# A hybrid decoder layer on one core: the recording clock learns the shared SBUF port and a measured matmul time, and every rank is set anew

## The chip, the core and the metric

The kernel runs on one core of a Trainium2 chip. The core has five engines that work from queues of their own, each strictly in the order in which its instructions were recorded: TensorE (PE in the profile, with its weight loads as PEld), VectorE (DVE), ScalarE (ACT), GpSimd (POOL) and SyncE (SP), which issues the DMA transfers. The metric is the device time of one execution in microseconds. The kernel before takes 1484.05 us, the median of three runs from 1482.07 to 1484.79.

## The reference, cut to what matters

One decoder layer is computed for a new sequence of 1024 tokens and for 8 single tokens that continue cached sequences (the sample). All data are float32.

```
h    = rmsnorm(x)
proj = h @ w_in                                # 1024 x 2336
y_r  = rwkv7_mix(proj[:, :1696])               # 8 heads x 64, state update over time
y_a  = windowed attention(proj[:, 1696:])      # 8 query heads, 2 KV heads, window 128, sinks
x    = x + concat(y_r, y_a) @ w_out            # 1024 x 1024
hf   = rmsnorm(x)
x    = x + relu(hf @ w_ffn_up)**2 @ w_ffn_down # 1024 x 4096, 4096 x 1024
```

The outputs are x for all tokens, and the new states and caches of both groups.

## The kernel before, in words

**Precision by two parts.** Each float32 operand of a dense product is split into a rounded high part and the rest: `whi` is made by ACT from a loaded weight tile `wraw`, `wlo` is the difference, made by DVE or POOL; for activations the pairs are `hh`/`hl`, `xu`/`xu`, `uh`/`ul`. One dense product is three matmuls, high by high, low by high and high by low, summed in PSUM. Weights come in halves of 128 x 512; there are 480 halves in all, in one fixed order. A raw ring of five and rings of three for `whi` and `wlo` stand between the transfer and the matmul.

**Stages.** The 1032 columns (1024 prompt tokens, 8 sample tokens) are four chunks of 256 (the last 264). For each chunk the stream `s_dense` computes the input projection (its first part is `lora`, then `pairs` and `kvq`). Its results feed three other streams: the RWKV recurrence in eight blocks d (`s_front`, `s_solve`, `s_X`, `s_back`, `s_rest`), attention (`s_cons`, `s_attn`), and the sample. Then `s_dense` computes the output projection of chunk 0, a first pass of the FFN over chunk 0 alone (256 columns at a time, tiles `xu`), the output projection of chunks 1 to 3, and the remaining FFN over the other 776 columns in pieces of 388. Norm statistics of chunk 1 are taken early, by `ssq_rs`: ACT squares the tiles `xk`, POOL adds them up in `ssq`, PE reduces them in `ps_m`.

**What sets the order.** The kernel is written as some twenty Python generators (streams), each of which yields instructions one by one. `drive` merges them: at every step it takes, of all streams' next instructions, the one that can start first by a clock of its own; among those that would start on the same engine before it has ended, it takes the one whose stream has the lower rank. Ranks are the numbers in `R`, capped by `BOOST` when the dense stream can't start soon. The clock keeps one busy time per engine (`busy`), the time at which each tile was written (`wrote`) and read (`used`), a latency between each pair of engines (`LAT`), and for each kind of instruction a cost by its size (`tt`, `ts`, `stt`, `cp`, `act`, `burst` for matmuls). It also counts matmul work in ticks of 3.41 us (`ticks`) and doubles the cost of a matmul when the tick before had too little; `hot`, with `HOT` and `HOT0`, puts the dense stream ahead of all others until the current tick has its share. This clock decides nothing at run time: its result is five fixed queues. Where a stream may choose the engine for a `wlo`, it takes POOL when POOL's clock is behind DVE's by a set margin.

Semaphore waits follow from the data. An instruction that stands in a queue ahead of its time holds everything behind it on that engine.

Of the kernel before, what the change touches and what calls it, by code (L numbers as in the profile page):

```python
# [167 lines left out]
}  # L168


PAD = 0.0
HOT = 1
HOT0 = 0.2
MR = 2
TICK = 10.24 / 3
SWITCH = 0.095
# [3 lines left out]
DB = -0.5  # L180
LIM = dict(x=1, d=3, ffn=4, e=4, o=1, f=2, a=4, y=1)
SLACK = 2
BOOST = dict(s_wl=2.5, s_w=2.5, mix_load=2.51, s_hprep=0.5, s_evac=0, s_post=0.1, s_phase=0.0, norm=0, s_dense=2.5, s_cons=2.5, s_back=2.5, decode=1.5, s_attn=1.56, sample=99, s_rest=0.16, s_X=99)
R = dict(s_back=1.96, s_X=1.24, s_solve=7.69, s_front=0, s_rest=6.92, s_evac=0.9, s_hprep=3.47, s_post=1.1, s_cons=0, s_w=0, s_wl=0.19, s_attn=6.24, s_dense=8.9, s_phase=7.55, mix_load=5.54, sample=5.41, decode=1.62, blocks=8.2, norm=2.24)
WIN = []
ENG = lambda nc: (nc.tensor, nc.vector, nc.scalar, nc.gpsimd, nc.sync)

# [1 line left out]
def build(tc, A, stop=None):  # L189
    nc = tc.nc  # L190
    V, S, G, T, SP = nc.vector, nc.scalar, nc.gpsimd, nc.tensor, nc.sync
# [9 lines left out]
    busy = {V: 0.6, S: 0.6, G: 0.6, T: 0.6, SP: 0.6}  # L201
    wrote, used, slots = {}, {}, {}

    def tl(pl, shape, tag=None, bufs=1, name=None, dtype=F32):
        kw = dict(tag=tag, bufs=bufs) if tag else {}
        t = pl.tile(shape, dtype, name=name or tag, **kw)
        if tag:
            old = slots.setdefault((id(pl), tag), [])
            if len(old) == bufs:
                used[t.name] = slot_use(old.pop(0))  # L210
            old.append(t.name)
        return t

    def slot_use(n):
        u = dict(used.get(n, {}))
        if n in wrote:
            u[wrote[n][1]] = max(u.get(wrote[n][1], 0.0), wrote[n][0])
        return u
# [3 lines left out]
    def names(aps):  # L222
        out = []
        for a in aps:
            if not hasattr(a, "name"):
                continue
            if a.name in wide:
                o = a.offset
                out += [f"{a.name}/{c}" for c in (1, 2, 3) if o < QS[c][0] + QS[c][1] - NQ and QS[c][0] - NQ < o + size(a)]
            else:  # L230
                out.append(a.name)
        return out

    def op(e, cost, outs, ins, fn, rows=128):
        return e, cost, names(outs), names(ins), fn, rows

    ticks, dmas, shape = {}, [0.0], [None]
# [16 lines left out]
    def start(o):  # L254
        e, cost, outs, ins = o[:4]
        t = busy[e]
        for n in ins:
            w = wrote.get(n)
            if w:
                t = max(t, w[0] + LAT[w[1], e] + (PAD if e is T and w[1] is not T else 0.0))  # L260
        for n in outs:
            for f, w in used.get(n, {}).items():
                t = max(t, w + LAT[f, e])
        return t

    order = (T, V, S, G, SP)
    LAT = {(x, y): v for x, row in zip(order, ((0.0, .2, .27, .2, .2),
# [6 lines left out]
    def do(*ops):  # L274
        for o in ops:
            t = start(o)
            e, cost, outs, ins, fn, rows = o
            fn()
            end = finish(e, t, cost, rows)
            busy[e] = t + 0.5 if e is SP else end  # L280
            for n in outs:
                wrote[n] = (end, e)
                if e in (V, G, S):
                    used.setdefault(n, {})[e] = end
            for n in ins:
                used.setdefault(n, {})[e] = end

    def size(a):
        n = 1
        for d in a.shape[1:]:  # L290
            n *= d
        return n
# [6 lines left out]

    def tt(e, out, a, b, o, more=0.0):  # L300
        c = 0.07 + size(out) / 960 if e is V else 0.1 + size(out) / 450 if o != POW else 0.25 + size(out) / 6
        return op(e, c + more, [out], [a, b], lambda: e.tensor_tensor(out=out, in0=a, in1=b, op=o))  # L302

    def ts(e, out, a, s1, op0, s2=None, op1=None):
        kw = {} if op1 is None else dict(op1=op1)
        c = 0.07 + size(out) / 1300 if e is V else 0.1 + size(out) / 700
        return op(e, c, [out], [a, s1, s2],
                  lambda: e.tensor_scalar(out=out, in0=a, scalar1=s1, scalar2=s2, op0=op0, **kw))

    def stt(out, a, s, b, op0, op1):  # L310
        return op(V, (0.13 if hasattr(s, "name") else 0.07) + size(out) / 960, [out], [a, s, b],
                  lambda: V.scalar_tensor_tensor(out=out, in0=a, scalar=s, in1=b, op0=op0, op1=op1))  # L312

    def cp(e, out, in_):
        c = 0.07 + size(out) / 1200 if e is V else 0.1 + size(out) / 280
# [15 lines left out]
    def burst(*calls):  # L331


        t, free, now, first, active, outs, ins, fns = 0.0, {}, None, None, 0.0, [], [], []
        end = 0.0
        for call in calls:
            turn = len(call) == 3
            out, l, r = call[:3]
            start, stop, shared = (True, True, False) if turn else (*call[3:], False)[:3]
            k, m, n = l.shape[0], (size(r) if turn else size(l)), (l.shape[0] if turn else size(r))  # L340
            one = turn or r.dtype == F32R
            sh = (edge(k), edge(m))
            step = max(n * (1 if one else 2) / 2400 + (0.0112 if one and not turn else 0.003), m / 1200 + 0.004, 0.027)
            where = (l.start_partition() if sh[0] < 128 else 0, out.start_partition() if sh[1] < 128 else 0)
            if now != sh:
                if now is not None:
                    t = end + SWITCH
                now, free = sh, {}
            first = first or sh
            for _ in range(1 if one else 2):  # L350
                t = max(t + 0.007, free.get(where, 0.0))
                free[where] = end = t + step
                end = max(free.values())
            active += 0.055 if turn else (n / 2400 if one else 2 * n / 2400) * k / 128
            outs.append(out)
            ins += [l, r]
            fns.append((lambda o=out, i=l, d=r: T.transpose(o, i, d)) if turn else
                       (lambda o=out, a=l, b=r, x=start, y=stop, z=shared: T.matmul(o, a, b, start=x, stop=y, skip_group_check=z)))  # L358

        def run():  # L360
            for f in fns:
                f()
        return op(T, end, outs, ins, run, (first, now, active))
# [13 lines left out]
    streams, done = [], {}  # L377
# [22 lines left out]
    def drive():  # L400
        windows, over = list(WIN), {}
        while streams:
# [6 lines left out]
            i = int(busy[T] / TICK)  # L409
            hot = ticks.get(i, 0.0) >= 3060 / 2400 * min(1.0, HOT * (busy[T] / TICK - i) + HOT0)  # L410

            eff = {}

            def base(s):
# [3 lines left out]
                r = over.get(n, s[0])  # L418
                return min(BOOST.get(n, 99), r) if low else r

# [34 lines left out]
    pp_ = cm.__enter__()  # L455
    own, held, free_at = {}, {}, [{} for _ in range(7)]

    def get(kind, shape, name):
        yield lambda on=HOLD.get(kind): held.get(kind, 0) < LIM[kind] and len(own) < 7
        i = min((i for i in range(7) if i not in own.values()), key=lambda i: max(free_at[i].values(), default=0.0))  # L460
        t = tl(pp_, shape, f"b{i}", 1, name)
        own[t.name] = i
        kinds[t.name] = kind
        held[kind] = held.get(kind, 0) + 1
        return t
# [12 lines left out]
        free_at[i] = slot_use(t.name)  # L478

    def pt(shape, tag, name):  # L480
        return tl(pp_, shape, tag, 1, name)

    const = es.enter_context(pool("const", "left"))
    dram = es.enter_context(pool("dram", space=bass.MemoryType.DRAM))
# [89 lines left out]
    def s_wl():  # L574
        for j, (src, M) in enumerate(halves):
            yield lambda on="s_w": len(his) > j
            lo = tl(wp, [128, 4, M], "wl", WH, "wlo", F32R)
            e = G if busy[G] + 1.3 < busy[V] + 0.6 and not done.get("solving") else V
            yield tt(e, lo, raws[j], his[j].bitcast(F32), SUB)
            W.append((his[j], lo))  # L580

# [891 lines left out]
    def sample(sp):  # L1473
# [82 lines left out]
        for i, E in enumerate((V, G)):  # L1556
            St2 = tl(sp, [128, 4, 64], "p9t" if i else "St", 1)
            t3 = tl(sp, [128, 4, 64], name=f"t3_{i}")
            spawn(R["blocks"], blocks(i, E, St2, t3, kk, z, bvec, v, kn, r, sa, y))
        yield lambda: done.get("blk") == 2  # L1560
# [93 lines left out]
    def out_proj(c):  # L1654
# [3 lines left out]
        def consumer(m):  # L1658
            def f(n, ps):
# [8 lines left out]
                if m == 7:  # L1668
                    spawn(R["norm"], norm(c, ssq))
            return f  # L1670
# [85 lines left out]
    def s_phase():  # L1756
        yield lambda on="s_post": done.get(("kvq", 3)) and done.get("post", 0) == 56
        hs_.close()
        bm[0] = es.enter_context(pool("bm", "left"))
        spawn(R["sample"], sample(es.enter_context(pool("smp", "left"))))  # L1760
        yield lambda on="s_front": done.get(("front", 7))
        rfs.close()
        new_act0()
        done["acts"] = 1
        spawn(R["mix_load"], mix_load(0))
        yield lambda on="s_solve": done.get("xs")
        rss.close()
        yield lambda on="s_cons": done.get("cons") == 24
        dec = ExitStack()
        spawn(R["decode"], decode(dec.enter_context(pool("dec", "right"))))  # L1770
        yield lambda on="decode": done.get("decode")
# [6 lines left out]
        done["acts"] = 2  # L1778
        spawn(R["mix_load"], mix_load(1))
        yield lambda on="s_rest": done.get(("tail", 7))  # L1780
# [155 lines left out]
```

## Time and profile before

| | |
|---|---|
| median of the runs | 1484.05 us (1482.07 to 1484.79) |
| the profiled execution | 1479.39 us, span of its instructions 1477.6 us |
| PE busy | 1379.6 us, 93% of the span |
| DVE, ACT, POOL busy | 862.6, 659.0, 610.2 us |
| mean granted TensorE clock | 0.965 |
| moved by DMA | 168.14 MB, mean 114 GB/s |

The page gives busy time by engine, the groups of instructions that cost most, and for idle time what ended it. The view by stretches cuts the span into pieces and gives each engine's busy time in each, with the granted clock; the view in order of time gives single instructions with the idle time before them in square brackets. A matmul counts as busy from its issue to its modelled end, so that PE looks busy when matmuls follow each other without a gap.

### The profile page before, as it was taken

Reading aid. Unit: us, or ns where it says so; the run is one execution under the profiler, and the core shown is the slowest. Engines: PE = TensorE matmul, PEld = TensorE weight load, DVE = VectorE, ACT = ScalarE, POOL = GpSimd, SP = SyncE. Lnnn points to the kernel's source line nnn. Section 1 sums busy time; section 2 is a strip of 40 time slices with the busy share of each in tenths; the row PEclk is TensorE's granted clock in tenths of the full one; section 3 lists DMA queues with packets and bytes.
Section 4 is the critical chain, followed back from the end, with each engine's and each line's share of the span. In section 5 each row is a group of like instructions: output and inputs, shape, how many; then the busy total and the mean of one; then the engine's idle time right before and its main releaser. Section 6 shows DMA issues by size and latency. Waiting matters only on the chain.

```text
span 1477.6 us, 31265 instructions
## 1 busy us (share of the span) xinstructions
PE 1379.6 (93%) x11798; PEld 1294.2 (88%) x11798; DVE 862.6 (58%) x1962; ACT 659.0 (45%) x1519; POOL 610.2 (41%) x909
## 2 busy tenths in 40 slices
PE   6898988899879988989889999999999999999999
PEld 5887777688768877779889988999999999999998
DVE  3777777758777786689976588333323323233323
ACT  4557655565566545456445555323231313222221
POOL 4676445744765553245644443222212121222221
PEclk7998999899999998999999999999999999999999
DMA  6445335434432445258656665422222222222223
GB/s 193 139 121 137 111 87 131 121 95 113 121 109 77 104 114 165 71 154 271 199 165 187 186 206 151 116 60 62 65 58 65 65 58 65 65 65 62 60 58 101
DMA packets 140918, 168.14 MB, mean 114 GB/s; under 512 B 49321, under 2 KB 75457, under 8 KB 140751
## 3 DMA queue, kind: packets, MB, share of 16 engines
q1 hardware_dynamic: 140766, 166.14, 39.5%
q8 instruction: 93, 1.52, 0.4%
q14 instruction: 59, 0.48, 0.1%
HBM read 150.13 MB, written 14.35 MB: 111 GB/s over the span
## 4 chain that ended last, share of the span: by engine, by line
PE 64%; DVE 15%; POOL 6%; DMA 6%; issue 4%; ACT 3%; SPq 2%; DVEq 0%; POOLq 0%; ACTq 0%
PE ps_d L358 56%; DVE wlo L302 2%; SPq L372 2%; POOL wlo L302 1%; DVE AT L302 1%; POOL xt L302 1%; ACT whi L298 1%; DMA Ms<-ms 1%; DMA qr<-qw 1%; POOL Xs L302 1%; DVE hf L312 1%; PE ps_o L358 1%; PE py L358 1%; DVE bk L302 1%; PE ps_s L358 1%
## 5 line engine op out<-in xcount | busy, mean ns | idle before, releaser
L302 POOL TENSOR_TENSOR wlo<-wraw,whi 128x512 fp32r<-128x512 f32 (+1 forms) x234 | 307.9, 1316 | 708.3 <-ACT whi L298 679.9
L298 ACT ACTIVATE whi<-wraw 128x512 fp32r<-128x512 f32 (+1 forms) x480 | 297.9, 624 | 482.8 <-PE ps_d L358 387.6
L302 DVE TENSOR_TENSOR wlo<-wraw,whi 128x512 fp32r<-128x512 f32 (+1 forms) x246 | 181.8, 743 | 146.7 <-ACT whi L298 146.2
L302 DVE TENSOR_TENSOR x<-ps_d,x 128x256 f32<-128x256 f32 (+2 forms) x352 | 119.6, 372 | 205.2 <-PE ps_d L358 204.3
L358 PE MATMUL ps_d<-hh,whi 128*128 128x256 f32 (+3 forms) x640 | 194.8, 304 | 14.4 <-ACT whi L298 8.0
L358 PE MATMUL ps_d<-hl,whi 128*128 128x256 f32 (+3 forms) x640 | 194.9, 305 | 6.3 <-DVE hl L302 3.6
L358 PE MATMUL ps_d<-hh,wlo 128*128 128x256 f32 (+3 forms) x640 | 196.8, 307 | 2.7 <-DVE wlo L302 1.8
L358 PE MATMUL ps_d<-wh,wlo 128*128 128x388 f32 x512 | 174.0, 340 | 0.0
L358 PE MATMUL ps_d<-wl,whi 128*128 128x388 f32 x512 | 173.8, 340 | 0.0
L358 PE MATMUL ps_d<-ul,whi 128*128 128x388 f32 x512 | 173.6, 339 | 0.0
L358 PE MATMUL ps_d<-wh,whi 128*128 128x388 f32 x512 | 173.6, 339 | 0.0
L358 PE MATMUL ps_d<-uh,wlo 128*128 128x388 f32 x512 | 173.5, 339 | 0.0
L358 PE MATMUL ps_d<-uh,whi 128*128 128x388 f32 x512 | 173.1, 338 | 0.0
L358 PEld LDWEIGHTS ps_d<-hh,whi 128*128 128x128 f32 (+1 forms) x640 | 124.8, 195 | 21.7 <-ACT whi L298 8.9
L358 PEld LDWEIGHTS ps_d<-hl,whi 128*128 128x128 f32 (+1 forms) x640 | 124.7, 195 | 13.8 <-DVE hl L302 4.7
L358 PEld LDWEIGHTS ps_d<-hh,wlo 128*128 128x128 f32 (+1 forms) x640 | 124.8, 195 | 9.8 <-DVE wlo L302 3.1
L358 PE MATMUL ps_d<-xu,whi 128*128 128x256 f32 x512 | 97.2, 290 | 2.7 <-ACT xu L298 1.6
L358 PE MATMUL ps_d<-ah,wlo 128*128 128x256 f32 x320 | 93.0, 291 | 5.9 <-DVE wlo L302 3.6
L358 PEld LDWEIGHTS ps_d<-wl,whi 128*128 128x128 f32 x512 | 96.3, 188 | 0.0
L358 PEld LDWEIGHTS ps_d<-wh,wlo 128*128 128x128 f32 x512 | 96.2, 188 | 0.0
L358 PEld LDWEIGHTS ps_d<-wh,whi 128*128 128x128 f32 x512 | 96.2, 188 | 0.0
L358 PEld LDWEIGHTS ps_d<-uh,wlo 128*128 128x128 f32 x512 | 96.1, 188 | 0.0
(333 smaller groups left out, 2966.6 us busy)
## 6 DMA issues: line engine op xcount, KB each, us to landing
wraw<-in_w_in SPq DMA_DIRECT2D x152, 256.0 KB
wraw<-in_w_up SPq DMA_DIRECT2D x128, 256.0 KB
wraw<-in_w_down SPq DMA_DIRECT2D x128, 256.0 KB
wraw<-in_w_out SPq DMA_DIRECT2D x64, 256.0 KB
x<-in_xT SPq DMA_DIRECT2D x16, 256.0 KB
xk<-in_xT SPq DMA_DIRECT2D x32, 128.0 KB
x<-mixd SPq DMA_DIRECT2D x16, 256.0 KB
xk<-in_xT SPq DMA_DIRECT2D x16, 132.0 KB
```

The source lines that it names most:

```text
L298: lambda: S.activation(out=out, in_=in_, func=func, **kw))
L302: return op(e, c + more, [out], [a, b], lambda: e.tensor_tensor(out=out, in0=a, in1=b, op=o))
L312: lambda: V.scalar_tensor_tensor(out=out, in0=a, scalar=s, in1=b, op0=op0, op1=op1))
L358: (lambda o=out, a=l, b=r, x=start, y=stop, z=shared: T.matmul(o, a, b, start=x, stop=y, skip_group_check=z)))
L372: return op(SP, 1.1 + 4e-6 * out.shape[0] * size(out) / 0.36, [out], [in_], lambda: SP.dma_start(out, in_))
```

## The change

Three things change in the clock, one in the choice of engine, and all tuned numbers.

1. An instruction of DVE or POOL whose operands all lie in SBUF is marked `"sbuf"` (`ports`, with the set `psums` of PSUM tiles): `tt` on both engines, `ts` on DVE alone, `stt`. If one is to start while the other engine's last marked instruction is running, its start is moved to that one's end.
2. A dense matmul of n columns costs n/2276 + 0.0065 us where it cost n/2400 + 0.0112 (and 0.119 where it was 0.118 for 256 columns, 0.177 where it was 0.173 for 388). `PAD` adds 0.03 us to each wait of PE for another engine, and `HOT0` goes from 0.2 to 0.3.
3. A `wlo` goes to POOL when POOL's clock is 1.09 us behind DVE's; before, 0.7 us (1.3 less 0.6).
4. Most numbers in `R`, and three in `BOOST`, are others.

No instruction is added or removed: PE has 9716 matmuls in both programs, ACT 1456 instructions, SP 878. 54 `wlo` of 128 x 512 go from POOL to DVE (240 to 294 on DVE, 232 to 178 on POOL), one small `wlo` goes the other way and three `hl` go from POOL to DVE.

```diff
-PAD = 0.0
+PAD = 0.03
 HOT = 1
-HOT0 = 0.2
+HOT0 = 0.3
...
-BOOST = dict(s_wl=2.5, ..., s_phase=0.0, ..., decode=1.5, s_attn=1.56, sample=99, s_rest=0.16, s_X=99)
-R = dict(s_back=1.96, s_X=1.24, s_solve=7.69, s_front=0, s_rest=6.92, s_evac=0.9, s_hprep=3.47, ..., s_wl=0.19, s_attn=6.24, ..., sample=5.41, decode=1.62, blocks=8.2, norm=2.24)
+GW = 1.09
+BOOST = dict(s_wl=2.5, ..., s_phase=0, ..., decode=1.36, s_attn=1.56, sample=99, s_rest=0, s_X=99)
+R = dict(s_back=2.73, s_X=5.89, s_solve=7.24, s_front=0, s_rest=7.46, s_evac=0.9, s_hprep=2.39, ..., s_wl=8.97, s_attn=5.31, ..., sample=5.62, decode=3.98, blocks=5.16, norm=3.48)
...
+        if o[5] == "sbuf":
+            a, b = port[V if e is G else G]
+            if a <= t < b:
+                t = b
         return t
+
+    port, psums = {V: (0.0, 0.0), G: (0.0, 0.0)}, set()
+
+    def ports(*aps):
+        return None if any(hasattr(a, "name") and a.name in psums for a in aps) else "sbuf"
...
             busy[e] = t + 0.5 if e is SP else end
+            if rows == "sbuf":
+                port[e] = t, end
...
-            step = max(n * (1 if one else 2) / 2400 + (0.0112 if one and not turn else 0.003), m / 1200 + 0.004, 0.027)
+            step = max(n / 2276 + 0.0065 if one and not turn else n * (1 if one else 2) / 2400 + 0.003, m / 1200 + 0.004, 0.027)
...
-            e = G if busy[G] + 1.3 < busy[V] + 0.6 and not done.get("solving") else V
+            e = G if busy[G] + GW < busy[V] and not done.get("solving") else V
```

What that does to the queues is shown at three places.

On ACT at the start of the program, where the weights of the first projection (`whi`) and the squares for the norm of chunk 1 (`ssq`, `sq`, from the tiles `xk` that a transfer brings) share the queue. Before:

```order
L298 ACTIVATE hh_292<-hf 128x256
L298 ACTIVATE ssq<-xk 128x256
L298 ACTIVATE sq<-xk 128x256 x2
L298 ACTIVATE whi<-wraw 128x512 x2
L298 ACTIVATE sq<-xk 128x256 x4
L298 ACTIVATE whi<-wraw 128x512 x2
L298 ACTIVATE P<-ps_d 32x256
```

And of the change:

```order
L310 ACTIVATE whi<-wraw 128x512 x2
L310 ACTIVATE hh_304<-hf 128x256
L310 ACTIVATE ssq<-xk 128x256
L310 ACTIVATE sq<-xk 128x256 x2
L310 ACTIVATE whi<-wraw 128x512 x2
L310 ACTIVATE P<-ps_d 32x256
L310 ACTIVATE P<-ps_d 128x256
L310 ACTIVATE sq<-xk 128x256
L310 ACTIVATE whi<-wraw 128x512
L310 ACTIVATE sq<-xk 128x256
L310 ACTIVATE whi<-wraw 128x512
```

Two more `whi` stand ahead of the first square, and the later squares stand one by one between the `whi`, where four stood in a row.

On PE at the same place, the two reductions of those squares (`ps_m`), each a pair of matmuls with one column. Before, they stood in the second full column of the projection:

```order
L358 MATMUL ps_d<-hh_265,whi 128x256
L358 MATMUL ps_d<-hl_266,whi 128x256
L358 MATMUL ps_m_434<-cst,ssq 128x1
L358 MATMUL ps_d<-hh_265,wlo 128x256
L358 MATMUL ps_d<-hh_274,whi 128x256
```

Of the change they stand 81 dense matmuls later:

```order
L370 MATMUL ps_d<-hh_304,whi 128x256
L370 MATMUL ps_d<-hl_305,whi 128x256
L370 MATMUL ps_m_573<-cst,ssq 128x1 x2
L370 MATMUL ps_d<-hh_304,wlo 128x256
L370 MATMUL ps_d<-hh_221,whi 128x256
```

Counted in dense matmuls ahead of them on PE (there are 7296), the first has 62 before and 143 now; the first block's `pz` in `s_front` has 170 before and 297 now.

On DVE in the first FFN pass, about where the 267th half of the weights is split (`r` and `xu` are the activation's square and its low part, `x_0_0` the residual sum, `St`, `t` and `s_` the sample's RWKV state and its temporaries). Before:

```order
L302 TENSOR_TENSOR wlo<-wraw,whi 128x512
L312 SCALAR_TENSOR_TENSOR r<-ps_d,r 128x256
L302 TENSOR_TENSOR xu<-r,xu 128x256
L302 TENSOR_TENSOR wlo<-wraw,whi 128x512
L312 SCALAR_TENSOR_TENSOR r<-ps_d,r 128x256
L302 TENSOR_TENSOR xu<-r,xu 128x256
L302 TENSOR_TENSOR x_0_0_8503<-ps_d,x_0_0_8503 128x256 x2
```

And of the change:

```order
L314 TENSOR_TENSOR wlo<-wraw,whi 128x512
L314 TENSOR_TENSOR xu<-r,xu 128x256
L314 TENSOR_TENSOR t_0_11198<-St,s_8403 128x256
L335 TENSOR_REDUCE s_sa<-t_0_11198 128x4
L324 SCALAR_TENSOR_TENSOR r<-ps_d,r 128x256
L314 TENSOR_TENSOR St<-St,s_z 128x256
L314 TENSOR_TENSOR wlo<-wraw,whi 128x512
L314 TENSOR_TENSOR xu<-r,xu 128x256
L314 TENSOR_TENSOR t_0_11198<-s_sa,s_8403 128x256
L314 TENSOR_TENSOR St<-St,t_0_11198 128x256
L324 SCALAR_TENSOR_TENSOR r<-ps_d,r 128x256
L335 TENSOR_REDUCE s_sa<-t_1_11200 128x4
```

The sample's state steps have come in between; before, they stood between halves 160 and 255, now nearly all between 240 and 295. In the halves from 240 to 311 DVE makes 48 of the 72 `wlo`, before 37. By groups of halves, POOL's share goes from 57 to 46 in the first 176, from 51 to 42 up to 288, from 24 to 20 up to 336, and from 102 to 73 in the last 144.

More of the change, by code (lines that the diff above doesn't have):

```diff
@@ L182 @@
 SLACK = 2
-BOOST = dict(s_wl=2.5, s_w=2.5, mix_load=2.51, s_hprep=0.5, s_evac=0, s_post=0.1, s_phase=0.0, norm=0, s_dense=2.5, s_cons=2.5, s_back=2.5, decode=1.5, s_attn=1.56, sample=99, s_rest=0.16, s_X=99)
-R = dict(s_back=1.96, s_X=1.24, s_solve=7.69, s_front=0, s_rest=6.92, s_evac=0.9, s_hprep=3.47, s_post=1.1, s_cons=0, s_w=0, s_wl=0.19, s_attn=6.24, s_dense=8.9, s_phase=7.55, mix_load=5.54, sample=5.41, decode=1.62, blocks=8.2, norm=2.24)
+GW = 1.09
+BOOST = dict(s_wl=2.5, s_w=2.5, mix_load=2.51, s_hprep=0.5, s_evac=0, s_post=0.1, s_phase=0, norm=0, s_dense=2.5, s_cons=2.5, s_back=2.5, decode=1.36, s_attn=1.56, sample=99, s_rest=0, s_X=99)
+R = dict(s_back=2.73, s_X=5.89, s_solve=7.24, s_front=0, s_rest=7.46, s_evac=0.9, s_hprep=2.39, s_post=1.1, s_cons=0, s_w=0, s_wl=8.97, s_attn=5.31, s_dense=8.9, s_phase=7.89, mix_load=2.45, sample=5.62, decode=3.98, blocks=5.16, norm=3.48)
 WIN = []
@@ L232, in names, with op @@
         return out
-    def op(e, cost, outs, ins, fn, rows=128):
+    def op(e, cost, outs, ins, fn, rows=None):
         return e, cost, names(outs), names(ins), fn, rows
@@ L301, in tt @@
         c = 0.07 + size(out) / 960 if e is V else 0.1 + size(out) / 450 if o != POW else 0.25 + size(out) / 6
-        return op(e, c + more, [out], [a, b], lambda: e.tensor_tensor(out=out, in0=a, in1=b, op=o))
+        return op(e, c + more, [out], [a, b], lambda: e.tensor_tensor(out=out, in0=a, in1=b, op=o), ports(out, a, b))
     def ts(e, out, a, s1, op0, s2=None, op1=None):
@@ L307, in ts @@
         return op(e, c, [out], [a, s1, s2],
-                  lambda: e.tensor_scalar(out=out, in0=a, scalar1=s1, scalar2=s2, op0=op0, **kw))
+                  lambda: e.tensor_scalar(out=out, in0=a, scalar1=s1, scalar2=s2, op0=op0, **kw), ports(out, a) if e is V else None)
     def stt(out, a, s, b, op0, op1):
         return op(V, (0.13 if hasattr(s, "name") else 0.07) + size(out) / 960, [out], [a, s, b],
-                  lambda: V.scalar_tensor_tensor(out=out, in0=a, scalar=s, in1=b, op0=op0, op1=op1))
+                  lambda: V.scalar_tensor_tensor(out=out, in0=a, scalar=s, in1=b, op0=op0, op1=op1), ports(out, a, b))
     def cp(e, out, in_):
@@ L462, in get @@
         own[t.name] = i
+        psums.add(t.name)
         kinds[t.name] = kind
@@ L480, in pt @@
     def pt(shape, tag, name):
-        return tl(pp_, shape, tag, 1, name)
+        t = tl(pp_, shape, tag, 1, name)
+        psums.add(t.name)
+        return t
     const = es.enter_context(pool("const", "left"))
```

## The prediction, on record before the run

> **What bounds the kernel now.** I read the page's busy times first, then the view by stretches, then the waits of PE, then the start in order of time.
>
> ```profile
> PE 1379.6 (93%) x11798; PEld 1294.2 (88%) x11798; DVE 862.6 (58%) x1962; ACT 659.0 (45%) x1519; POOL 610.2 (41%) x909
> ```
>
> PE is idle for 98 of 1477.6 us. The stretches (us; busy and count of PE, PEld, DVE, ACT, POOL; then clock, DMA) show where; I cut at the end of the start, at the output projection of chunk 0, at the first FFN pass and its fully covered middle, and at the long FFN.
>
> ```profile
> 0.00:46.00 46.00, 31.95 (x188) 28.84 (x189) 21.12 (x37) 22.23 (x50) 24.51 (x50) 0.81 0.63 189
> 46.00:546.00 500.00, 445.94 (x5354) 390.25 (x5352) 377.03 (x878) 294.83 (x768) 286.87 (x574) 0.94 0.42 112
> 546.00:619.00 73.00, 67.65 (x854) 54.19 (x854) 47.07 (x138) 33.28 (x95) 26.60 (x48) 0.93 0.43 125
> 619.00:765.00 146.00, 130.86 (x1056) 121.54 (x1055) 128.73 (x275) 75.35 (x169) 78.65 (x82) 0.96 0.63 191
> 765.00:850.00 85.00, 85.00 (x720) 84.86 (x720) 52.95 (x94) 46.49 (x89) 38.71 (x30) 1.00 0.62 184
> 850.00:917.00 67.00, 61.27 (x479) 58.09 (x479) 56.32 (x108) 40.04 (x90) 29.70 (x30) 0.99 0.61 185
> 917.00:1477.60 560.60, 556.93 (x3159) 556.39 (x3159) 179.36 (x435) 146.82 (x264) 125.18 (x97) 0.99 0.24 69
> ```
>
> From 917 us on PE never waits, with 3159 matmuls in 556.93 us (176 ns each) and DVE busy a third of the time. Their number and shape stay, so nothing there can be won or, with that much room, lost: the 29 `wlo` that DVE takes over there add 29 x 0.69 = 20 us to its 179 of 560. All that can change lies before 917 us. PE idles there for 14.1, 54.1, 5.4, 15.1, 0 and 5.7 us, 94 in all, and its clock is below full: (1 - 0.81) x 46 + 0.06 x 500 + 0.07 x 73 + 0.04 x 146 = 50 us of pulses missing, part of them while PE was idle anyway. No plan gets all of this back; the change is a new plan of the same instructions, so I price it stage by stage.
>
> **The start (term A).** PE's and ACT's instructions in order of time (start, duration; idle time before and what ended it in brackets), and three stretches:
>
> ```profile
> 31.05 0.39 PE L358 MATMUL ps_d<-hh,whi 128*128 128x256 f32 x1 [3.83 <-ACT whi L298]
> 34.10 0.58 PE L358 MATMUL ps_m<-cst,ssq 128*128 128x1 f32 x2 [2.55 <-POOL ssq L302]
> ```
>
> ```profile
> 22.32 0.42 ACT L298 ACTIVATE sq<-xk 128x256 f32<-128x256 f32 x1 [0.28 <-POOL ssq L302]
> 29.73 0.76 ACT L298 ACTIVATE sq<-xk 128x256 f32<-128x256 f32 x2 [6.98 <-DMA xk<-in_xT]
> 30.39 1.14 ACT L298 ACTIVATE whi<-wraw 128x512 fp32r<-128x512 f32 x2
> ```
>
> ```profile
> 28.64:32.05 3.41, 0.50 (x2) 0.30 (x2) 1.02 (x2) 2.32 (x7) 1.69 (x2) 1.00 0.46 120
> 32.05:35.47 3.42, 1.36 (x6) 1.37 (x7) 1.74 (x2) 1.90 (x5) 2.10 (x6) 0.50 0.75 199
> 35.47:38.88 3.41, 3.41 (x18) 3.41 (x17) 2.36 (x4) 2.87 (x7) 3.27 (x6) 0.50 0.32 95
> ```
>
> Two heads of a queue hold PE. ACT stands 6.98 us at a square whose `xk` hasn't landed, with the next two `whi` behind it; PE runs dry for 3.83 us. Then PE stands 2.55 us at `ps_m`, which needs the same late squares, with dense matmuls behind it whose data are there. And after the stretch with 0.50 us of PE work the clock is halved for the next two: their 1.36 + 3.41 us of work at half clock cost 2.4 us more. Together 3.83 + 2.55 + 2.4 = 8.8 us. The change puts two more `whi` ahead of the squares, spreads the squares between the `whi`, and puts `ps_m` 81 dense matmuls later, some 10 us at 119 ns. The second stall should go. Of the first something may stay, as the late `xk` still holds one `whi` at a time, and the transfers of two weight halves now stand ahead of the fourth `xk` on SP. Bounds: 0 and -8.8; I take -5. What is late for it is the first block of the recurrence (127 dense matmuls, some 15 us) and chunk 1's norm; the latter is wanted at the 480th dense matmul; the recurrence's last matmul has 2388 dense ones ahead of it (2292 before), and the output projection that wants its result begins after some 3600. So neither has PE waiting.
>
> **The sample's steps and the first FFN pass (terms B and C).** DVE's rows for the sample's state, and for `wlo` up to 917 us and after (min/median/max ns):
>
> ```profile
> L302 DVE TENSOR_TENSOR St<-St,t x8: 406/420/1518, 676.7 to 744.1; 128x256 f32<-128x256 f32 x8
> L323 DVE TENSOR_REDUCE s_y<-t x8: 405/410/420, 693.5 to 756.1; 128x4 f32<-128x256 f32 x8
> ```
>
> ```profile
> L302 DVE TENSOR_TENSOR wlo<-wraw,whi x210: 278/691/1790, 10.3 to 915.2; 128x512 fp32r<-128x512 f32 x104, 128x128 fp32r<-128x128 f32 x1
> L302 POOL TENSOR_TENSOR wlo<-wraw,whi x137: 453/1291/2272, 9.3 to 912.7; 128x512 fp32r<-128x512 f32 x135, 128x128 fp32r<-128x128 f32 x2
> L302 DVE TENSOR_TENSOR wlo<-wraw,whi x36: 691/693/695, 921.1 to 1440.5; 128x512 fp32r<-128x512 f32 x36
> ```
>
> About 48 such steps on DVE, 48 x 0.41 = 20 us, leave the stretch to 765 us, where DVE is busy 88%, for the halves 240 to 295, most of which lie in the covered stretch behind it. There they meet 11 more `wlo`, 11 x 0.69 = 7.6 us. For PE, a late `wlo` is the largest item in these stretches:
>
> ```profile
> PE ps_d L358 <- DVE wlo L302: 7.8, 10, 2.1
> PE ps_d L358 <- POOL wlo L302: 3.0, 3, 2.4
> ```
>
> B: the sum of these, 10.8 us, is the most that a freer DVE returns; at worst nothing. Since the sample's attention moves into the place left free, I take half, -5. C: the covered stretch goes from 52.95 to 52.95 + 20 + 7.6 = 80.6 of 85 us on DVE. Its least price is 0 (DVE still fits), its highest what the stretch before pays at 88%: 15.1/146 of 85 us idle, 8.8, and 4% of clock, 3.4, so 12. I take +3, nearer to the row with room, since the steps spread beyond 85 us.
>
> **The middle (term D).** PE's longest waits from 46 to 546 us (total, times, longest):
>
> ```profile
> PE pA L358 <- DVE ar L302: 8.6, 5, 2.6
> PE pH L358 <- ACT UV L298: 4.5, 5, 2.6
> PE pcum L358 <- DVE sg L308: 4.2, 4, 1.4
> PE ps_d L358 <- DVE hl L302: 3.6, 2, 2.7
> PE pbn L358 <- DVE o L312: 3.5, 1, 3.5
> PE pb_k L358 <- POOL hrs L302: 3.1, 3, 2.5
> ```
>
> They are few and long, where the plan had the operand ready and the chip did not. One cause of such misses is the port. The same `wlo` takes 691 to 695 ns late in the program and up to 1790 early, and in time:
>
> ```profile
> 228.92 1.78 DVE L302 TENSOR_TENSOR wlo<-wraw,whi 128x512 fp32r<-128x512 f32 x1
> ```
>
> ```profile
> 228.78 1.37 POOL L302 TENSOR_TENSOR wlo<-wraw,whi 128x512 fp32r<-128x512 f32 x1
> ```
>
> DVE's began 0.14 us after POOL's and took 1.78 - 0.69 = 1.09 us too long, about what POOL's had left. The old clock had no such wait, the new one has. But knowing it doesn't remove it; it only lets the order fit. D has no row of its own: at best the new order returns the five DVE and POOL items quoted, 23.0 us; at worst it loses as much, since every rank is new and the old order had been fitted to its own misses. I take -3.
>
> The new matmul cost (119 ns for 118) and `PAD` move positions by a few matmuls; they have no price apart from D. `HOT0` neither: dense work comes a little sooner in each tick, and the halved clock of the middle (30 us of pulses) lies within D's bounds.
>
> The clock's port is not complete. POOL's `ts` and its copies are not marked, and the trace has them wait:
>
> ```profile
> L308 POOL TENSOR_SCALAR Pa<-P,dv x56: 469/482/1317, 32.9 to 513.3; 128x256 f32<-128x256 f32 x39, 128x264 f32<-128x264 f32 x13, 32x256 f32<-32x256 f32 x3, 32x264 f32<-32x264 f32 x1
> ```
>
> One of 0.48 us took 1.32. I leave D at -3, because an unmarked 0.48 us holds DVE less long than a `wlo` of 1.29. The Trainium skill's page "SBUF — State Buffer", section "Who interferes with whom", says that a VectorE instruction with two SBUF inputs contends with any GpSimd instruction that reads SBUF. That speaks against the change as it is made: by it, an order fitted to some of the contention still misses at the rest, and D would be 0, the sum -7 and the median 1477. The trace agrees that such instructions are held, by the row above; how often DVE is held by them it doesn't show.
>
> The sum: -5 - 5 + 3 - 3 = -10 us against the profiled execution's 1479.4, so 1469.4; the median of the runs lies 4.7 above that execution, so 1474 for the median.
>
> **The rivals.** *Slower: DVE becomes the bound in the first FFN pass.* Place: 765 to 850 us, where PE has no gap now. For it: 80.6 of 85 us of DVE work by the sum above, more with port waits, of which a `wlo` or a step each can be one; in the stretch at 88% PE already idles. Against it: at 62% PE did not wait once, and the raw and split rings let `wlo` run three halves ahead. It decides when DVE's work in the stretch passes PE's 85 us. Price: C at +12, with A's -5 kept and B and D at 0: 1484 + 7 = 1491.
>
> *No change.* The losses move but stay as many: A's 5 us go to other first stalls, B and C cancel, D is 0. For it: 94 us of idle in many small pieces is what five fixed queues leave, whatever the ranks. Time 1484. This is also how it goes if the clock doesn't know the port well enough: the 39 and more unmarked `Pa` above stand in the middle, the stage with the most idle time.
>
> *Much faster: the middle was the clock's fault.* If the port was what made the plan miss, all 23.0 us of D return, with their share of halved clock (30/54 of it, of which half is work: 6): -5 - 5 + 3 - 29 = -36, so 1448. Against it: ACT's waits are in the same list, and the port can't be behind these.
>
> **How the numbers follow.** Forecast (-10): 0.46. Much faster: 0.12. No change: 0.16. Slower: 0.26. Less than 0.2%, 3 us, counts as no change here, so faster is 0.46 + 0.12 = 0.58, same 0.16, slower 0.26. The forecast's own range is 1463 to 1481: downward each term goes half way to its bound and they add as independent errors (1.9, 2.9, 1.5 and 10 give 11), upward it ends where no change begins. The range for the time reaches past the slower rival's 1491 by 4 and, downward, half way from the forecast's own end to its furthest, 1454 with D at -23: 1458 to 1495. That leaves out most of the much faster case, 0.1, and a third of the slower one, 0.09.
>
> **What would show it.** A: no idle of over 2 us before a `ps_d` or `ps_m` between 25 and 40 us, full clock from 32 us. B and C: in 619 to 765 us PE idle below 12 us, in the 85 us behind it DVE at 85 to 95% and PE still over 97%. D: PE idle in the middle at 45 to 55 us. The last 557 us: 3159 matmuls in the same time within 1 us. The prediction is wrong if the middle's idle moves by over 15 us either way, or if `wlo` heads PE's waits with over 20 us.

## The result and the profile after

The kernel after takes 1439.25 us (median of four runs, 1435.99 to 1441.52) where the kernel before takes 1483.06 (four runs, 1475.67 to 1484.79): a ratio of 0.9712, 95% interval 0.9671 to 0.9753. The gain is 43.8 us; the forecast had 10, and its range ended at 1458. The direction was right and the size was not. The profiled execution took 1441.52 us, its span is 1439.7, against 1477.6 before: 37.9 us are to be found in the two traces (the rest is where the two profiled executions lie in their runs: 3.7 us below the median before, 2.3 above it after).

The busy times of the page after:

```profile
PE 1368.0 (95%) x11798; PEld 1288.9 (90%) x11798; DVE 879.2 (61%) x2018; ACT 657.1 (46%) x1519; POOL 546.4 (38%) x853
```

PE is idle for 71.7 us (98.0 before) and busy for 11.6 us less with the same 11798 instructions, at a mean granted clock of 0.974 where it was 0.965. The stretches after, cut where PE has reached the same dense matmuls as at the prediction's cuts (137, 1903, 2079, 2971, 3687 and 4138 of 7296 ahead), with the columns of the view shown there:

```profile
0.00:34.40 34.40, 29.16 (x181) 26.56 (x182) 17.24 (x32) 17.81 (x41) 17.68 (x36) 0.95 0.70 220
34.40:518.30 483.90, 436.71 (x5322) 385.22 (x5322) 380.87 (x891) 295.77 (x773) 278.69 (x571) 0.96 0.43 117
518.30:578.40 60.10, 56.17 (x726) 47.24 (x726) 43.66 (x124) 30.96 (x86) 26.12 (x51) 0.91 0.52 147
578.40:725.00 146.60, 142.02 (x1218) 130.95 (x1217) 107.92 (x248) 78.72 (x180) 60.21 (x58) 0.94 0.59 179
725.00:818.40 93.40, 88.42 (x723) 85.95 (x722) 76.67 (x152) 45.97 (x89) 47.34 (x43) 1.00 0.65 190
818.40:880.50 62.10, 59.93 (x481) 57.83 (x479) 53.88 (x109) 40.56 (x88) 28.48 (x28) 1.00 0.67 201
880.50:1439.70 559.20, 555.56 (x3159) 555.16 (x3158) 198.93 (x466) 147.35 (x265) 87.91 (x68) 1.00 0.24 69
```

| stretch before | length before, after | PE idle before, after | forecast |
|---|---|---|---|
| start, 0 to 46 | 46.0, 34.4 (-11.6) | 14.1, 5.2 | A -5 |
| middle, 46 to 546 | 500.0, 483.9 (-16.1) | 54.1, 47.2 | D -3 |
| 546 to 765 | 219.0, 206.7 (-12.3) | 20.5, 8.5 | B -5 |
| 765 to 850 | 85.0, 93.4 (+8.4) | 0.0, 5.0 | C +3 |
| 850 to 917 | 67.0, 62.1 (-4.9) | 5.7, 2.2 | none |
| the rest | 560.6, 559.2 (-1.4) | 3.7, 3.6 | 0 |

PE's longest waits in the middle after (total, times, longest), which answer to the list shown before:

```profile
PE pH L370 <- ACT UV L310: 7.4, 8, 2.1
PE ps_d L370 <- DVE wlo L314: 6.0, 5, 3.2
PE ps_d L370 <- DVE hl L314: 5.0, 5, 2.5
PE ps_d L370 <- ACT whi L310: 4.8, 3, 4.4
...
PE pA L370 <- DVE ar L314: 1.6, 1, 1.6
```

Of the five DVE and POOL items that bounded D, `pA` fell from 8.6 to 1.6, and `pcum`, `pbn` and `pb_k` have left the head of the list; `hl` stands at 5.0 (3.6 before), and a `wlo` item of 6.0 has come in. So the waits were not taken away evenly: one list of few and long waits was exchanged for another, with 47.2 us of idle time for 54.1. The wait for ACT's `UV` rose from 4.5 to 7.4.

At the start, PE's only wait of over 0.3 us between 25 and 39 us, and ACT's queue (start, duration, idle time before in brackets):

```profile
36.53 0.61 PE L370 MATMUL ps_m<-cst,ssq 128*128 128x1 f32 x4 [1.30 <-POOL ssq L314]
```

```profile
24.54 0.62 ACT L310 ACTIVATE P<-ps_d 32x256 f32<-32x256 f32 x2
25.29 0.42 ACT L310 ACTIVATE sq<-xk 128x256 f32<-128x256 f32 x1
25.62 0.61 ACT L310 ACTIVATE whi<-wraw 128x512 fp32r<-128x512 f32 x1
26.14 0.40 ACT L310 ACTIVATE sq<-xk 128x256 f32<-128x256 f32 x1
```

The squares find their `xk`; the 6.98 us in front of a square are gone, and so are the 3.83 and 2.55 us on PE.

### The profile page after: what moved, and what is told of

Its sections match the earlier page's. It is cut to its first block, busy times and chain, and to the rows that moved or that the text cites. A ratio compares the mean times of both kernels' runs of the same rounds, so it can differ in the third digit from the quotient of the medians.

```text
span 1439.7 us, 31186 instructions
## 1 busy us (share of the span) xinstructions
PE 1368.0 (95%) x11798; PEld 1288.9 (90%) x11798; DVE 879.2 (61%) x2018; ACT 657.1 (46%) x1519; POOL 546.4 (38%) x853
## 4 chain that ended last, share of the span: by engine, by line
PE 50%; DVE 5%; issue 1%; DMA 1%; POOL 0%; ACT 0%; DVEq 0%; SPq 0%; POOLq 0%
PE ps_d L370 49%; DVE wlo L314 2%; DMA St<-in_state 1%; DVE t L314 1%; DVE St L314 1%; DVE x L314 1%; DVE wl L314 1%; POOL wlo L314 0%; DVE hf L324 0%; DVE xu L314 0%; DVE r L324 0%; PE pb_f L370 0%; DVE ssq L314 0%; PE ps_pt L369 0%; PE py L370 0%
## 5 line engine op out<-in xcount | busy, mean ns | idle before, releaser
L314 POOL TENSOR_TENSOR wlo<-wraw,whi 128x512 fp32r<-128x512 f32 (+1 forms) x181 | 240.8, 1331 | 712.8 <-ACT whi L310 692.4
L314 DVE TENSOR_TENSOR wlo<-wraw,whi 128x512 fp32r<-128x512 f32 (+1 forms) x299 | 218.1, 731 | 132.5 <-ACT whi L310 129.0
L370 PE MATMUL ps_d<-hh,wlo 128*128 128x256 f32 (+3 forms) x640 | 193.3, 302 | 7.5 <-DVE wlo L314 6.3
L370 PE MATMUL ps_d<-hl,whi 128*128 128x256 f32 (+3 forms) x640 | 192.0, 300 | 7.6 <-DVE hl L314 5.0
L370 PEld LDWEIGHTS ps_d<-hh,wlo 128*128 128x128 f32 (+1 forms) x640 | 123.5, 193 | 13.5 <-DVE wlo L314 8.0
L370 PE MATMUL ps_d<-ah,whi 128*128 128x256 f32 x320 | 94.2, 294 | 2.5 <-ACT ah L310 2.5
```

## The experiments

Beside times, a second number is used here: the end that a kernel's own recording clock gives to its list while the list is made ("plan"). It is the number by which ranks can be compared without a chip, and the distance from it to the span of the profiled execution ("miss") says how well the clock knows the chip. All spans are cut at the 144th, 2112th and 4140th dense matmul of 7296: start, middle, first FFN pass, rest. A span is that of one profiled execution, which can lie off the median that the ratio is made of: furthest above it with the new ranks under the old clock (1508.47 for a median of 1496.92), furthest below it for the kernel searched on (1435.79 for 1439.59). Differences of a few us between spans are within that.

| run | ratio, 95% interval | span: start + middle + FFN 1 + rest | plan | miss |
|---|---|---|---|---|
| before | 1 | 46.9 + 590.7 + 280.2 + 559.8 = 1477.6 | 1412.3 | +65 |
| after | 0.971 (0.967 to 0.975) | 37.3 + 559.5 + 284.3 + 558.6 = 1439.7 | 1429.4 | +10 |
| new clock, old ranks | 0.999 (0.996 to 1.003) | 36.6 + 589.7 + 292.4 + 557.5 = 1476.2 | 1487.2 | -11 |
| old clock, new ranks | 1.012 (1.004 to 1.019) | 44.9 + 619.4 + 283.4 + 559.0 = 1506.7 | 1439.4 | +67 |
| after without the port rule | 1.010 (1.003 to 1.017) | 33.5 + 611.3 + 291.2 + 557.5 = 1493.5 | 1437.6 | +56 |
| after, old `PAD` and `HOT0` | 0.990 (0.984 to 0.996) | 46.6 + 577.7 + 281.1 + 557.5 = 1463.0 | 1463.8 | -1 |
| after, old margin for POOL | 0.976 (0.973 to 0.979) | 34.5 + 583.7 + 272.9 + 557.5 = 1448.5 | 1447.5 | +1 |
| after, ranks disturbed | 0.990 (0.987 to 0.992) | 36.0 + 594.3 + 277.0 + 557.5 = 1464.8 | 1466.7 | -2 |
| before, ranks disturbed | 1.017 (1.013 to 1.020) | 47.2 + 615.5 + 289.3 + 557.5 = 1509.6 | 1456.1 | +53 |
| before, no `wlo` on POOL | 0.982 (0.978 to 0.985) | 45.8 + 581.9 + 273.3 + 557.7 = 1458.7 | 1432.9 | +26 |
| before, new `PAD` alone | one execution, 1475.96 us | 33.4 + 589.3 + 291.6 + 559.9 = 1474.1 | 1427.5 | +47 |
| after, fuller port rule | 0.978 (0.975 to 0.981) | 35.4 + 577.4 + 273.4 + 559.1 = 1445.3 | 1456.1 | -11 |
| fuller rule, own ranks | 0.959 (0.951 to 0.967) | 33.8 + 558.6 + 270.6 + 557.5 = 1420.6 | 1411.4 | +9 |
| after, searched on | 0.976 (0.969 to 0.982) | 38.7 + 561.0 + 276.8 + 557.5 = 1434.0 | 1418.7 | +15 |

### The clock alone, the ranks alone, the port rule off

The first takes the kernel after with the old `R` and `BOOST`; the second the kernel before with the new ones; the third turns off one test in the kernel after.

```diff
-R = dict(s_back=2.73, s_X=5.89, ..., norm=3.48)      # the kernel after
+R = dict(s_back=1.96, s_X=1.24, ..., norm=2.24)
```

> The changed kernel with R and BOOST of before: the new clock, matmul cost, port, PAD, HOT0 and margin, but the old ranks. If the better clock makes the gain (it lets any order fit the chip), most of the 44 us remain: 1440 to 1455. If the new ranks make it, it comes out near before: 1475 to 1495. If only the pair does (ranks found under the clock that they are used with), also 1475 or more, and then the ranks alone must fail too.

```diff
-R = dict(s_back=1.96, s_X=1.24, ..., norm=2.24)      # the kernel before
+R = dict(s_back=2.73, s_X=5.89, ..., norm=3.48)
```

> The kernel before with R and BOOST of the change alone: the old clock, margin 0.7, HOT0 0.2. If the ranks make the gain: 1440 to 1450. If the clock makes it: 1475 to 1490. If only the pair does: 1470 or more.

```diff
-        if o[5] == "sbuf":                             # the kernel after
+        if False:
```

> The changed kernel, but the clock takes no account of the shared port; the matmul cost, margin and ranks are those of the change. If knowing the port is what makes the order fit: at least 15 us of the 44 are lost, 1455 or more. If the port's part is small (my term D, -3): within 6 us of the change, 1439 to 1446.

Measured: 1478.36 us, no change against before; 1496.92, slower by 1.2%; and 1496.15, slower by 1.0%. Neither half of the change has the gain, only the pair has it. The third run leaves the new ranks, the new matmul cost, `PAD`, `HOT0` and the margin where they are, and without the port rule the kernel after loses 57 us. Any edit under numbers that were found for another setting may cost something (the next runs: 9 to 29 us), but here the clock's own plan is only 8 us worse than that of the kernel after (1437.6 for 1429.4); the rest of the 54 us of span is a larger miss. Its busy times, and three middles: its own, that of the new ranks under the old clock, and that of the kernel after (the columns are those of the view by stretches):

```profile
PE 1381.4 (92%) x11798; PEld 1300.1 (87%) x11798; DVE 890.7 (60%) x2009; ACT 654.8 (44%) x1519; POOL 550.6 (37%) x862
```

```profile
33.50:644.80 611.30, 530.15 (x6291) 462.91 (x6289) 454.20 (x1072) 339.56 (x901) 316.62 (x635) 0.92 0.39 110
```

```profile
44.90:664.30 619.40, 546.20 (x6370) 475.58 (x6368) 446.18 (x1070) 338.11 (x894) 318.65 (x629) 0.89 0.39 110
```

```profile
37.30:596.80 559.50, 507.37 (x6173) 444.43 (x6173) 436.63 (x1053) 332.04 (x876) 306.59 (x622) 0.95 0.43 119
```

In the first two PE is idle for 81 and 73 us of the middle, at a granted clock of 0.92 and 0.89. In the kernel after, with the same ranks, it is idle for 52 us at 0.95. No engine but PE is busy for more than three quarters of these stretches: what is lost is lost to order. And both plans were wrong by some 60 us, as was that of the kernel before, and as none was under the port rule.

One rival to all of this wasn't tried: new ranks searched under the old clock for as long as the change's were under the new one. So it is shown that these ranks need this clock, and not that no ranks under the old clock could have had the gain.

### Other numbers under either clock

Is the plan believable for other numbers too, or did the kernel after just hit a good set? Three edits of the kernel after and two of the kernel before: `PAD` 0.03 to 0 with `HOT0` 0.3 to 0.2; the margin `GW` 1.09 to 0.7; each rank moved at random by up to 2, in either kernel; and `PAD` 0 to 0.03 in the kernel before.

> The changed kernel with PAD 0 and HOT0 0.2 as before. If these have no price of their own, as predicted: within 6 us of the change. If any edit of a number under ranks that were found for another setting costs, as a rank that fits one clock alone would: 1450 to 1475, with the idle time of PE up by 10 us or more.

> The changed kernel with the margin for POOL at 0.7 us as before (GW), all else as changed. If the margin matters by the number of wlo on POOL: a few us, 1440 to 1448. If any edit under ranks found for another setting costs what the new clock says of it: its own end is 1447 (the change's 1429), so 1450 to 1465.

> The changed kernel with each rank moved at random by up to 2; the new clock ends at 1467 us with them (1429 with the change's). If the new clock tells the chip's time, within 15 us: 1455 to 1482. If it is no better than the old one, 1500 or more; if ranks hardly matter under it, 1440 to 1450.

> The kernel before with each rank moved at random by up to 2; the old clock ends at 1456 us with them (1412 with before's own). If the old clock misses the port's 50 to 65 us whatever the ranks: 1506 to 1525. If before's ranks were only bad luck on the chip: 1465 to 1490.

> The kernel before with PAD 0.03 alone. In the runs so far the 144th dense matmul starts at 47 us where PAD and HOT0 are old and at 34 to 37 us where they are new, whatever the ranks and the port. If PAD makes that: below 38 us here, and the span 5 to 10 us less than it would be; the old clock ends 15 us later with this order (1427 for 1412), so with its miss of 55 to 65 us the whole is 1480 to 1493. If HOT0 makes it: 45 to 48 us.

Measured: 1465.28, 1448.29, 1467.92 and 1508.16 us; of the last kernel the profiled execution alone is used, 1475.96 (the one other took 2129 us, at a granted clock of 0.555). Under the port rule the plans 1429, 1447, 1464, 1467 and 1487 stand in the same order as the spans 1440, 1448, 1463, 1465 and 1476, and each is met within 11 us (what that hides comes below; a list that was searched on under this rule, further below, is missed by 15). Without the port rule the plans 1412, 1427, 1438, 1439 and 1456 became 1478, 1474, 1493, 1507 and 1510: all 47 to 67 us late. The kernel after is a good set among others, worth 9 to 29 us over its neighbours, and the clock with the port rule had ranked it first of them.

`PAD` alone, in this one execution, shows how a gain in one stage goes: the start is as short as with the whole change (33.4 us for 46.9), and the first FFN pass is 11.4 us longer (291.6 for 280.2), so that only 3.5 us are left of 13.5. The whole was expected at 1480 to 1493 and came out below that, with a miss of 47 us where 55 to 65 were expected. So `PAD`, which the forecast had put at no price, is enough for the start's gain, and that gain need not last through the later stages. `HOT0` alone and the old matmul cost in the kernel after weren't tried.

### Is it the port? The contention taken away

In the kernel before, no `wlo` goes to POOL any more; clock and ranks stay the old ones. DVE gets 234 more `wlo`.

```diff
-            e = G if busy[G] + 1.3 < busy[V] + 0.6 and not done.get("solving") else V
+            e = V
```

> The kernel before, but every wlo is made on DVE, so that POOL's largest group, the one that shares the port with DVE most, is gone; clock and ranks are those of before. By the old clock this order is 21 us worse than before's (its own end goes from 1412 to 1433 us, while before's span on the chip was 1478, 65 us later than its clock said). If the port is what the old clock misses, the chip ends at most 45 us after the clock: 1478 or less, as fast as before or faster, with 246 more DVE instructions less POOL's. If the miss has another cause (latencies, matmul cost), the 65 us stay and it takes 1495 to 1505.

Measured: 1455.93 us, faster by 1.8%, though the old clock calls this list 21 us slower than the one before (1432.9 for 1412.3). The page:

```profile
PE 1382.1 (95%) x11798; PEld 1295.5 (89%) x11798; DVE 944.1 (65%) x2197; ACT 659.3 (45%) x1519; POOL 309.6 (21%) x674
```

DVE's low part of the first FFN pass's activation, before and here (min/median/max ns):

```profile
L302 DVE TENSOR_TENSOR xu<-r,xu x32: 410/962/1514, 646.7 to 916.7; 128x256 fp32r<-128x256 f32 x32
```

```profile
L302 DVE TENSOR_TENSOR xu<-r,xu x32: 408/417/954, 637.5 to 900.2; 128x256 fp32r<-128x256 f32 x32
```

POOL loses 301 us of work and DVE gains only 82, though 234 x 0.69 = 161 us of `wlo` moved to it. Most of the difference is that DVE's other instructions got shorter, by 57 us in sum; the one shown went from 962 to 417 ns. The trace of the kernel before tells what ran beside the long ones. An instruction's quiet time is here the lower quartile of its group (same line, operands and shape). Counting instructions that took over 0.15 us more than that, DVE ran 87 us over in sum, and 84 of these belong to instructions that began while a `tensor_tensor` of POOL was running. In the run without POOL's `wlo` the 87 are 27.

The miss falls from 65 to 26 us. Counted at the 2112th dense matmul (from the first one on, in plan and trace), it falls from 65.5 to 43.0; between the kernel after without the port rule and with it, from 65.4 to 31.9. Taking the contention away thus does what putting it into the clock does. Up to there the port is shown to make a third to a half of the miss; the rest of it is open.

### The part of the port that the change leaves out

The change marks no `tensor_scalar` and no copy of POOL. Here both are marked; all numbers stay those of the kernel after.

```diff
-                  ..., ports(out, a) if e is V else None)
+                  ..., ports(out, a))
...
-        return op(e, c, [out], [in_], lambda: e.tensor_copy(out, in_))
+        return op(e, c, [out], [in_], lambda: e.tensor_copy(out, in_), ports(out, in_) if e is G else None)
```

> The changed kernel, whose clock also marks POOL's tensor_scalar and copies; ranks those of the change, so that they no longer fit. Its clock ends at 1456 us. With the change the chip ended 10 us after its clock, 32 late up to the end of the middle and 21 early after it. If the unmarked POOL instructions make those 32: the chip ends before the clock, 1435 to 1448. If they are too short to matter: 1460 to 1470, as late as before in the middle.

Measured: 1448.4 us, where 1435 to 1448 was expected if they make the 32. The list is 27 us worse by its plan and 6 us by its span, so the miss turns from +10 to -11. At the 2112th dense matmul the chip is 31.9 us behind the clock in the kernel after and 16.8 here. That these instructions make 15 us of the miss isn't shown by it, though: other lists under the narrower rule are missed by 20 us (old ranks) to 43 us (searched on) at the same place, and the one with the old ranks ends 11 us ahead of its clock as well.

What the trace of the kernel after does show is that an unmarked instruction holds DVE. This `wlo` of DVE, 0.69 us when quiet, began 0.11 us after POOL's `Pa` and took 0.90:

```profile
40.60 0.90 DVE L314 TENSOR_TENSOR wlo<-wraw,whi 128x512 fp32r<-128x512 f32 x1 [0.21 <-DMA wraw<-in_w_in]
```

```profile
40.49 0.48 POOL L320 TENSOR_SCALAR Pa<-P,dv 128x256 f32<-128x256 f32 x1 [0.46 <-DVE xq L324]
```

That agrees with what the prediction cited from the Trainium skill's page "SBUF — State Buffer", section "Who interferes with whom", that a VectorE instruction with two SBUF inputs contends with any GpSimd instruction that reads SBUF. In sum it is little on DVE's side: in the kernel after, its instructions that began during a `tensor_scalar` or copy of POOL ran 3 us over, while those POOL instructions themselves ran 23 us over.

With the clock made fuller, its numbers have to be found again. Two kernels: the fuller rule with `R`, `BOOST`, `GW`, `PAD` and `HOT0` searched under it by plan alone (`HOT0` stayed at 0.3), and, against it, the change's own rule with `R`, `BOOST` and `GW` searched on for about as long.

```diff
-PAD = 0.03                                             # fuller rule, own ranks
+PAD = 0.013
...
-GW = 1.09
+GW = 1.81
...
-R = dict(s_back=2.73, s_X=5.89, ..., s_wl=8.97, ..., norm=3.48)
+R = dict(s_back=2.33, s_X=6.07, ..., s_wl=2.89, ..., norm=2.43)
```

> The clock of e8_full_port (POOL's tensor_scalar and copies kept off VectorE's port time as well), with the numbers R, BOOST, GW, PAD and HOT0 searched anew under it: its own clock ends at 1411.4 us (the kernel after: 1429.4 under the narrower port rule, e8_full_port 1456.1). Theory (a list order is worth what its clock says, once the clock knows the port): the chip ends 0 to 11 us ahead of that clock, as it did in e8_full_port, 1400 to 1412 us, a ratio of 0.945 to 0.953. Rival (the change's gain was that one set of ranks, found by luck, and a search under a clock is worth nothing on the chip): a time among those of other ranks under these clocks, 1440 to 1470 us, ratio 0.97 to 0.99. Second rival (the clock is exploited by a search: its errors are collected by the ranks): the chip ends 20 to 40 us behind the clock, 1430 to 1450 us.

> The clock of the kernel after as it is (the narrow port rule), with R, BOOST and GW searched on under it, about as long as for e13_full_port_own_ranks: its own clock ends at 1418.7 us (the kernel after 1429.4, e13_full_port_own_ranks 1411.4 by the fuller rule, measured 1419). Theory (a search collects what its clock leaves out, and the narrow rule leaves out more, namely POOL's tensor_scalar and copies): the chip ends 18 to 35 us behind this clock, 1437 to 1454 us, no better than the kernel after. Rival (e13's gain over the kernel after came from searching longer, not from the fuller rule): the chip follows the clock as it did for the kernel after (+10) and e13 (+9), 1425 to 1431 us.

Measured: 1419.26 us (1413.55 to 1424.92), a ratio of 0.9589, with an interval of 0.951 to 0.9668 that lies below that of the kernel after; and 1439.59 (1435.79 to 1451.08), no better than the kernel after. The first beats both kernels. Its page and its middle:

```profile
PE 1357.2 (96%) x11798; PEld 1281.1 (90%) x11798; DVE 884.2 (62%) x2042; ACT 657.3 (46%) x1519; POOL 508.6 (36%) x829
```

```profile
33.80:592.50 558.70, 515.24 (x6328) 450.39 (x6327) 442.06 (x1077) 336.48 (x890) 297.13 (x618) 0.95 0.43 121
```

The expectation for it, 1400 to 1412, was missed by 7 us. The miss of +9, where the same clock with foreign numbers had -11, fits a search that collects the errors of its clock: at the 2112th dense matmul the chip is 34 us behind, with the numbers of the kernel after 17. Under the narrower rule it is 32 and 43 us behind for the two searched lists and 20 to 32 for the four others, and the plan that was searched on is 11 us better than that of the kernel after with nothing of it on the chip. That the fuller rule, and not the longer search, made the 20 us between the two medians isn't shown: each is one draw of a random search, and `PAD` was searched in the first alone. Nor does the gain lie where the unmarked `Pa` stand: of the 19 us of span between the first and the kernel after, 14 are in the first FFN pass (270.6 for 284.3), and the middle is the same (558.7 for 559.5).

## Why the prediction was wrong in size

**The step that failed is D: "knowing it doesn't remove it; it only lets the order fit", priced at -3 of ±23.** The price was not drawn from this sentence, which is true. The stages came out at -11.6 (A), -16.1 (D), -12.3 (B), +8.4 (C), -4.9 for a stretch that had no price and -1.4 for the last: -37.9 where the sum said -10. Of the 27.9 us between them D is the largest part, 13.1; B has 7.3, A 6.6, C 5.4 the other way, and the unpriced stretches 6.3.

The contention did stay: DVE's time above the quiet time of each of its groups is about 100 us before and 82 after, POOL's 69 in both. Two rows after, for DVE's and POOL's largest group:

```profile
L314 DVE TENSOR_TENSOR wlo<-wraw,whi x240: 279/691/1671, 10.6 to 909.9; 128x512 fp32r<-128x512 f32 x117, 128x128 fp32r<-128x128 f32 x3
L314 POOL TENSOR_TENSOR wlo<-wraw,whi x120: 452/1293/3747, 9.7 to 916.3; 128x512 fp32r<-128x512 f32 x117, 128x128 fp32r<-128x128 f32 x3
```

But what fitted was worth far more than 3 us: of the 53.8 us of span that the port rule makes with the new numbers, 51.8 lie in the middle up to the 2112th dense matmul (611.3 to 559.5; the kernel before has 590.7). The forecast treated the new numbers as a throw of dice around the old order. They are good numbers under a clock that misses less, and what the forecast lacked was the size of the old clock's error: its own end, 1412, stood 65 us under the profiled span. That says how far the plan was from the chip, not that the distance would be won: with the old ranks the new clock's list ends within 11 us of its plan and gains nothing. The forecast had named that error ("the plan had the operand ready and the chip did not") and then bounded it by five of the waits, without asking what the clock as a whole misses. The rival "much faster: the middle was the clock's fault" named the mechanism, was given 0.12, and its 1448 was itself 9 us short. "ACT's waits are in the same list, and the port can't be behind these" was the argument against it; ACT's largest wait even rose (4.5 to 7.4) while the stage became 16 us shorter. In the accounts by stage D is -16.1, within its bounds; 6.9 of it is idle time, the rest PE work that ran at the higher clock (0.96 for 0.94) and 32 matmuls that moved out of the stretch. The sign by which the forecast was to be judged, a middle with 45 to 55 us of idle time, came true at 47.2 and didn't tell the cases apart, since it left out the granted clock; neither of its two signs of being wrong came.

**A** was right in its place and its two stalls and too small: -11.6 for -5, beyond its bound of -8.8. The idle time alone fell by 8.8, where the bound had 6.4 of idle time and 2.4 of half clock; PE's busy time fell by another 2.8, with 7 matmuls fewer and a granted clock of 0.95 for 0.81. Of the signs asked for, no idle time of over 2 us is there; the full clock from 32 us lasted only to 35.4, with 0.74 in the next 3.4 us, behind the 1.30 us at `ps_m`. "They have no price apart from D" was wrong for `PAD`.

**B** was -5 within 0 to -10.8 and became -12.3: the idle time of its two stretches fell from 20.5 to 8.5 us, and PE's waits for a `wlo` there, the mechanism named, from 9.8 to 2.1 (128 matmuls that aren't dense left the first stretch and 162 more are in the second, so they are taken together). **C** had the right sign and load: DVE's work went from 52.95 to 76.67 us where 80.6 was forecast, and the stretch became 8.4 us longer, with 5.0 of idle time, within its 0 to 12. The slower rival's mechanism is thus there, at its place (3.7 of the 5.0 us are waits for DVE), and worth 8 us. DVE's share of 82% and PE's of 95% are just below those named. Rows of the stretch after, where the sample's steps meet POOL (us busy, mean ns):

```profile
L314 DVE TENSOR_TENSOR St<-St,t 128x256 f32<-128x256 f32 x6 | 5.3, 887 | 0.0
L314 DVE TENSOR_TENSOR t<-St,s_r 128x256 f32<-128x256 f32 x4 | 4.4, 1100 | 0.1
```

All eight of the first kind took 420 ns before in the median, and 894 now. The load on DVE is not a count of instructions by quiet durations: the step that moves meets the port at its new place.

**The last stretch** kept its 3159 matmuls and changed by 1.4 us, as said within about 1. DVE's 29 more `wlo` there cost 19.6 us of its time and nothing on PE.

The rule from the Trainium skill's page "SBUF — State Buffer", section "Who interferes with whom", agrees with the trace (the `wlo` beside a `Pa` above). The result drawn from it, D at 0, was wrong: a clock that knows part of the contention doesn't miss as before, it misses by less, 32 us instead of 65 at the 2112th dense matmul. That it ends only 10 us off is in part luck: from the 4140th dense matmul to the last, the new clock counts 575.6 us where the chip takes 554.6, and the old one counted 562.9 (the chip 555.8). The new matmul cost thus moves the plan's last stretch further away from the chip, and the 21 us too many there hide two thirds of what is still missed in the middle.

## What to carry to other kernels

Where a model sets a static order, compare the model's own end with the measured span first: the distance (65 us here, where the longest wait in the middle's list was 3.5) says how far the order may be fitted to something that isn't so. Mend the model and search its numbers again as one change, since either half alone gave nothing here (0.999 and 1.012), and expect a search to eat some of the model's accuracy. Compare model and trace stage by stage too, since two errors can cancel in the end time. A second engine that contends with the first isn't free capacity: try the same work on one engine before balancing it over two.

## What the runs showed of the hardware

Moving all of POOL's `wlo` to DVE made the kernel before 27 us faster, with POOL's busy time at 309.6 us for 610.2 and DVE's only 82 us longer; the load balance that the margin kept was a loss there. Contention lengthened instructions of either engine to more than twice the quiet time: POOL's `wlo` of 1.29 us took up to 3.75, DVE's of 0.69 up to 1.79, and POOL's `Pa`, which the change leaves unmarked, 0.48 us when quiet, took up to 2.13 in the fastest kernel, while three `wlo` of DVE ran beside it:

```profile
L320 POOL TENSOR_SCALAR Pa<-P,dv x56: 470/482/2127, 23.9 to 475.5; 128x256 f32<-128x256 f32 x39, 128x264 f32<-128x264 f32 x13, 32x256 f32<-32x256 f32 x3, 32x264 f32<-32x264 f32 x1
```
